# Three weight rings, alternating chunk products and earlier low-rank weights in an RWKV-7/Conformer block

## The chip, the cores and the metric

The kernel runs on one NeuronCore of a Trainium2 chip. The metric is the device time of one execution in microseconds (us). TensorE (PE) multiplies into PSUM, ScalarE (ACT) and VectorE (DVE) do the elementwise work, GpSimd (POOL) and SyncE (SP) issue transfers (DMA) between the chip's memory and SBUF.

## What is computed

One layer on x of 512 tokens by 1024 channels, in float32: a mixer of two branches, then a gated feed-forward network (FFN).

```
h = rms_norm(x); proj = h @ w_in                  # r, k, v, conv (2), z_rwkv, z_conv: 7 x 1024 columns
w = w0 + tanh(xw @ w1) @ w2;  a = sigmoid(a0 + (xa @ a1) @ a2);  g = sigmoid(xg @ g1) @ g2
...
S = S * w_t + (S @ a_t) b_t^T + v_t k_t^T;  y_t = S @ r_t          # wkv7: 16 heads of 64, over 512 steps
y_rwkv = (group_norm(y) + bonus) * g @ w_rwkv_out
y_conv = silu(layer_norm(depthwise_conv31(u * sigmoid(gate)))) @ w_conv_out
x = x + rms_norm((sigmoid(z_rwkv) * y_rwkv + sigmoid(z_conv) * y_conv) @ w_out)
h = rms_norm(x); f = (silu(h @ w_gate) * (h @ w_up)) @ w_down      # d_ff = 2816
x = x + rms_norm(f)
```

## The kernel before

**Products.** Channels lie on the partitions, the 512 tokens along the free axis. A float32 product is made of three products in the format fp32r: weights and data are each split into a high and a low part (`wh`, `wl`; `HH`, `HL`), and `acc3` adds `wh` by high, `wh` by low and `wl` by high. A product of 1024 inputs into 128 outputs ("a tile") thus takes 24 matmuls of 512 columns into one of two PSUM tiles `dn`; a tile of the down projection, with 2816 inputs, takes 66.

**Loads of weights.** A load is half a tile's weights: 128 by 512 numbers, 256 KB. `wload` (L436) knows two ways. By SP: a transfer into `wf`, ScalarE copies it into `wh`, VectorE subtracts and writes `wl` (`split`, L432). By POOL: a transfer into `wh`, ScalarE writes its negative into `wl`, and a second transfer adds the weights to `wl`. All of these tiles have the tag "w" in the pool `wp`, whose number of places is `WT` (12). `wres` (L1132) and `lastw` (L1342) take a `wf` of the same tag alone and split into tiles elsewhere that stay resident.

**The planned part.** Everything from the first keys to the last tile of `w_co` goes through the class `Sched`: it does not issue instructions at once, but collects them in streams, gives each a cost (`times`, L182), simulates the five engines and issues the instruction that can start first, by priority (a smaller number is more urgent). `order` then fixes this order for each engine. Products stand in `sc.items` as a tile with the events that it needs (`dense_tile`, L703); `feed` (L315) takes the first item in the list whose events are posted and keeps at most `WB` = 6 halves loaded ahead; all go through one stream "dense", in order. Loads go by SP until the event "open", then by POOL until the taps of the last convolution tile are planned, then by SP again.

For each pair of heads `ct` (0 to 7; two heads of 64 channels fill 128 partitions, `E` are the lower 64 rows, `O` the upper) there are `prep` (keys, decays, and `gps`: the products inside chunks of 64 tokens), `solve` (inverse of a triangular matrix, products on 16 and 32 rows such as `wqs`), `values`, `chain` (eight chunks, one after another) and `finish`. They call each other by events: `prep(ct)` posts ("keys", ct), ("tr", ct) and ("inner", ct), `values` posts ("val", ct). The tile of `v` for `ct` needs ("val", ct-1).

`gps` works in two halves `hc` of four chunks; in each it fills a PSUM tile for the head in `E` and then one for the head in `O` (both of the tag "sm", two places), four float32 products each of 64 rows, 128 outputs and 128 columns. Each PSUM tile is then read twice by ScalarE (into `Mt`) and twice by VectorE (into `AR`, `GR`).

`conv(ct)` makes two tiles (gate and value), `taps(ct)` the 31 taps of the depthwise convolution on VectorE. `norms` (L1086) writes the normalised input `HH`, `HL`, then splits the low-rank weights of g (`low_weights(1)`, into `wg`) and puts the item of `low_rank1` (48 matmuls `lora`) at the end of `sc.items`; when these are made, it posts "low1". The convolution tiles from `ct` = 1 on, and the taps, need "low1", because the tile "ca" first holds x, then `wg`, then the convolutions.

**The rest.** After `sc.run()` (L1234) the instructions are given in plain program order and the framework schedules them: five tiles of `w_o` (`dense`, L459), interleaved with `wres` for the first four gate/up tiles; three further tiles of `w_o` from resident weights; the residual and the first four gate/up tiles from resident weights (`psf`); 20 pairs of gate/up tiles (L1327); seven tiles of the down projection, with `lastw` for the eighth (L1355); the eighth tile in two halves of the tokens. For each pair of gate/up tiles VectorE does `sg` = gate * `bc`, ScalarE silu, VectorE `sg` * `bc` and `sg` * up, and ScalarE and VectorE split the result into `FH` (high and low). A down tile is evicted by ScalarE (`dn`, then its square).

The two ways of `wload` before the change:

```
if eng is G:
    wh, wl = (wp.tile([P, nk * P], F32R, tag="w", name=n_) for n_ in ("wh", "wl"))
...
    wf = wp.tile([P, nk * P], F32, tag="w", name="wf")
    wh, wl = (wp.tile([P, nk * P], F32R, tag="w", name=n_) for n_ in ("wh", "wl"))
```

Of the kernel before, what the change touches and what calls it, by code (L numbers as in the profile page):

```python
# [3 lines left out]

# [5 lines left out]
F32 = mybir.dt.float32  # L10
F32R = mybir.dt.float32r
# [6 lines left out]
P = 128  # L18
# [3 lines left out]
NT = D // P  # L22
# [7 lines left out]
KW = 31  # L30
WK = 4
WB = 6
WT = 12
LB = {"mu_r": 2, "mu_k": 2, "mu_v": 1}
NWO = 3
BUFS = (2, 2, 2, 2, 1, 1, 1)
# [45 lines left out]
def tile_hybrid_block(ctx, tc, xT, cst, prm, dwp, wl1, w2g, w_in, w_ro, w_co, w_o,  # L82
# [13 lines left out]
    class Sched:  # L96
# [85 lines left out]
        def times(self, eng, name, k, aps):  # L182

            out = aps[0]
            n = math.prod(out.shape[1:])
            if eng == "PE":
                lhsT, rhs = k["lhsT"], k["rhs"]
                n, m = math.prod(rhs.shape[1:]), math.prod(lhsT.shape[1:])
                if lhsT.dtype == F32R:
                    c = max(0.112, 0.452e-3 * n)  # L190
                elif name == "transpose":
                    c = 0.112
                elif m > 64:
                    c = 2 * max(0.112, 1.02e-3 * n)
                else:
                    c = 0.058 if m > 32 else 0.016
                return c, c + 0.17, 0.0
            if "dma" in name:
                size = P * n * 4 if out.shape[0] > 64 else 64 * n * 4
                land = 2.0 + size / 200e3  # L200
                if eng == "POOL":
                    return (0.91, 0.06, land + 0.7) if k.get("accum_op") else (0.65, 0.06, land + 0.3)
                return 0.06, 0.06, land
            psum = any(str(a.space) == "PSUM" for a in aps[1:])
            if eng == "ACT":
                t = 0.17 + 0.9e-3 * n - (0.03 if psum else 0)
                t += sum(0.08 for a in ("scale", "bias") if hasattr(k.get(a), "ap"))
                return t + 0.02, t, 0.0
            if eng == "POOL":
                return 0.2 + 1.2e-3 * n, 0.2 + 1.2e-3 * n, 0.0  # L210
            t = 0.16 + 1.035e-3 * n
            if name == "scalar_tensor_tensor":
                t += 0.05 if n > 64 else 0
            elif name == "transpose":
                t = 0.16 + 1.8e-3 * n
            elif name == "tensor_tensor_scan":
                t = 0.16 + 2.06e-3 * n
            elif name in ("tensor_scalar", "tensor_copy"):
                t = 0.15 + 0.75e-3 * n
            return t - 0.08, t, 0.0  # L220
# [139 lines left out]
    sc = Sched()  # L360
# [19 lines left out]
    PE, SY = Engine("PE", nc.tensor), Engine("SP", nc.sync)  # L380

    def pool(stack, name, bufs, **k):
        return Pool(stack.enter_context(tc.tile_pool(name=name, bufs=bufs, **k)), bufs)

    cp = pool(ctx, "cp", 1)
    wp = pool(ctx, "wp", WT)
    tp = pool(ctx, "tp", 1)
    sp = pool(ctx, "sp", 2)
    pd = pool(ctx, "pd", 2, space=PSUM)
    pm = pool(ctx, "pm", 2, space=PSUM)  # L390
# [38 lines left out]
    E, O = slice(0, 64), slice(64, 128)  # L429
# [5 lines left out]

    def wload(wap, nk, eng=None):  # L436
        if eng is G:
            wh, wl = (wp.tile([P, nk * P], F32R, tag="w", name=n_) for n_ in ("wh", "wl"))
            G.dma_start(out=wh, in_=wap)
            S.activation(out=wl, in_=f(wh), func=AF.Copy, scale=-1.0)  # L440
            with sc.stream("low"):
                G.dma_start(out=wl, in_=wap, accum_op=ALU.add)
        else:
            wf = wp.tile([P, nk * P], F32, tag="w", name="wf")
            wh, wl = (wp.tile([P, nk * P], F32R, tag="w", name=n_) for n_ in ("wh", "wl"))
            SY.dma_start(out=wf, in_=wap)
            split(wf, wh, wl)
        return wh, wl
# [200 lines left out]
    def low_rank1():  # L649
        t_ = low[1]  # L650
        d = {}

        def mm(k):
            if k == 0:
                d["ps"] = pd.tile([P, T], F32, tag="dn", name="lora")
            for q, rh, rl in ((0, hh, hl), (2, hhs, hls)):
                o = acc3(d["ps"], t_[:, q, k, :], t_[:, q + 1, k, :], [k], rh, rl,
                         k + q == 0, k == NT - 1 and q == 2)
            if k == NT - 1:
                lo_f = tmp("lo_f", "th")  # L660
                S.activation(out=lo_f, in_=d["ps"], func=AF.Tanh, scale=0.5)
                S.activation(out=lo_f, in_=lo_f, func=AF.Identity, scale=0.5, bias=0.5)
                split(lo_f, GH, GL)
                sc.post("low1")
            return o

        sc.items.append(((), lambda: [(lambda eng: None, [lambda k=k: mm(k) for k in range(NT)])]))

    def open_loop():
        nonlocal kp  # L670
# [75 lines left out]
    def prep(ct):  # L746
# [57 lines left out]
        AR = kp.tile([P, NCH, 3, L], F32, tag="AR", bufs=BUFS[0], name="AR")  # L804
        bk = kp.tile([P, NCH, 2 * L], F32, tag="bk", bufs=1, name="bk")
# [8 lines left out]
        for hc in range(2):  # L814
            ps = pm.tile([P, 4, P], F32, tag="sm", name="tps")
# [14 lines left out]
        GR = kp.tile([P, NCH, 2, L], F32, tag="GR", bufs=BUFS[1], name="GR")  # L830
        sm = lambda rows: m_str[rows].unsqueeze(1).to_broadcast([64, 4, L])
        for hc in range(2):
            for par in range(2):
                cc = slice(hc * 4, hc * 4 + 4)
                R, Q = ((E, O), (O, E))[par]
                ps = pm.tile([P, 4, P], F32, tag="sm", name="gps")
                for c in range(4):
                    PE.matmul(ps[:, c, :], lhsT=bk[R, hc * 4 + c, :],
                              rhs=AR[R, hc * 4 + c, par:3:2 - par, :], start=True, stop=True)
                r0 = R.start  # L840
                S.activation(out=Mt[r0:r0 + B32, cc, :], in_=ps[r0:r0 + B32, :, 0:L],
                             func=AF.Copy)
                S.activation(out=Mt[r0 + B32:r0 + L, cc, 0:B32],
                             in_=ps[r0 + B32:r0 + L, :, B32:L], func=AF.Copy)
                V.tensor_mul(AR[Q, cc, par, :], ps[Q, :, 0:L], sm(Q))
                V.tensor_mul(GR[:, cc, par, :], ps[:, :, L:2 * L],
                             m_inc.unsqueeze(1).to_broadcast([P, 4, L]))
# [183 lines left out]
    def conv(ct):  # L1031
        cv = {}

        def gate(ps):
            if ct == 0:
                ps = early(ps)
            cv["th"] = tmp("th")
            S.activation(out=cv["th"], in_=ps, func=AF.Tanh, scale=0.5)

        def value(ps):  # L1040
            if ct == 0:
                ps = early(ps)
            cb = conv_in[ct] = conv_place(ct) if ct else cpad0
            V.scalar_tensor_tensor(out=cb[:, KW - 1:], in0=cv["th"], scalar=1.0,
                                   in1=ps, op0=ALU.add, op1=ALU.mult)

        rh, rl = (hh, hl) if ct else ((lambda k: XH[:, k, :]), (lambda k: XL[:, k, :]))
        need = ("low1",) if ct else ()
        dense_tile(w_in[4 * NT + ct], gate, rh, rl, need)
        dense_tile(w_in[3 * NT + ct], value, rh, rl, need, ("cv", ct))  # L1050

# [34 lines left out]
    def norms():  # L1086
        normed()
        yield "rest"
        low_weights(1)
        low_rank1()  # L1090
# [15 lines left out]
    sc.fast = False  # L1106
    sc.spawn(once(first_keys), 2)
    sc.spawn(once(low_inputs), 1)
    sc.spawn(norms(), 3)
    conv(0)  # L1110
    for ct in range(1, NT):
        dense_tile(w_in[NT + ct], lerp_of("tk", D_OMK, "mu_k", ct), need=(("keys", ct - LB["mu_k"]),) if ct >= LB["mu_k"] else (),
# [2 lines left out]
                   need=(("val", ct - 2),) if ct > 1 else (), ev=("r", ct))  # L1115
# [16 lines left out]
    def wres(wap, hi, lo, j):  # L1132
        for k0 in range(0, NT, WK):
            c = slice(k0 * P, (k0 + WK) * P)
            o_ = slice(j * D + k0 * P, j * D + (k0 + WK) * P)
            wf = wp.tile([P, WK * P], F32, tag="w", name="wf")
            SY.dma_start(out=wf, in_=wap[:, c])
            split(wf, hi[:, o_], lo[:, o_])

# [81 lines left out]
    for m in range(NT):  # L1221
        dense_tile(w_in[6 * NT + m], lambda ps, m=m: gate_c(m, ps),
                   need=(("inner", NT - 1), ("val", NT - 1)))
# [25 lines left out]
    for m in range(NT - NWO):  # L1249
        ps = dense(w_o[m], mh, ml)  # L1250
# [91 lines left out]
    def lastw(i):  # L1342
        if i < 4:
            n = WK
            t_ = [kq.tile([P, WK * P], F32R, tag=QT[2 * i + h], bufs=QT.count(QT[2 * i + h]),
                          name="lw") for h in range(2)]
            wf = wp.tile([P, WK * P], F32, tag="w", name="wf")
            SY.dma_start(out=wf, in_=w_dn[NT - 1][:, i * WK * P:(i + 1) * WK * P])
            split(wf, *t_)
        else:  # L1350
            n = min(WK, NF - i * WK)
            t_ = wload(w_dn[NT - 1][:, i * WK * P:(i * WK + n) * P], n)
        last.append((n, *t_))

    for m in range(NT - 1):  # L1355
        ps = dense(w_dn[m], Fh, Fl)
# [7 lines left out]
    for h in range(2):  # L1364
        c = HALF[h]
        ps = pd.tile([P, TH], F32, tag="dn", name="dn")
# [82 lines left out]
```

## Time and profile before

| | |
|---|---|
| time, median of 3 runs | 1222.57 us (1222.13 to 1225.49) |
| profiled execution | 1221.62 us, its span 1219.6 us |
| busy share of the span | TensorE 91%, weight loads 72%, VectorE 61%, ScalarE 46%, GpSimd 8% |
| mean granted clock of TensorE | 0.958 of 2.4 GHz |
| transfers | 106.95 MB, mean 88 GB/s |

The span runs from the first to the last instruction of the profiled execution. Matmuls are pipelined and their ends are modelled, so that a busy TensorE is not one at its peak. The granted clock is a mean over a stretch; the clock itself has two levels, 1.2 and 2.4 GHz. Lines of the profile that end in brackets give the idle time of the engine just before the instruction and what ended it. In the planned part every instruction has the line L300, behind it L225, so that instructions are known by their tiles.

### The profile page before, as it was taken

The numbers are of one execution on the slowest core, as the hardware profiler recorded it, in microseconds if no ns is written. First come the engines' busy times: TensorE is split into PE (matmuls) and PEld (weight loads), VectorE is DVE, ScalarE is ACT, GpSimd is POOL, SyncE is SP. The second block draws the span as 40 slices with busy tenths as digits, with TensorE's granted clock in tenths as the row PEclk, the third lists the DMA queues.
The fourth block names the chain that finished last, engine by engine and source line by source line (L and its number), as shares of the span: only waits on it lengthen the run. The fifth ranks groups of instructions, "written<-read, shape, count | busy, mean of one in ns | idle before, by whom it ended". The sixth has DMA issues, their size and how long they took to land.

```text
span 1219.6 us, 18527 instructions
## 1 busy us (share of the span) xinstructions
PE 1115.1 (91%) x7066; PEld 883.2 (72%) x7066; DVE 741.5 (61%) x1507; ACT 562.7 (46%) x1199; POOL 100.3 (8%) x167
## 2 busy tenths in 40 slices
PE   6978999999999899899999998999988888888896
PEld 5756777777777677577788876988766666666676
DVE  6869888989899888867543553664443434412214
ACT  6456666667767665464742333542222222222211
POOL 0022222222122221000000000000000000000000
PEclk9888998989899998998999998999999999999998
DMA  6033544545354542222232243012222222322322
GB/s 236 22 74 72 118 81 93 113 92 111 71 111 81 125 88 55 67 84 87 83 99 95 95 144 98 18 44 92 91 69 86 69 87 70 92 79 81 91 72 69
DMA packets 68440, 106.95 MB, mean 88 GB/s; under 512 B 15104, under 2 KB 20608, under 8 KB 68352
## 3 DMA queue, kind: packets, MB, share of 16 engines
q1 hardware_dynamic: 49344, 71.16, 18.8%
q0 software_dynamic: 19008, 34.61, 14.1%
q8 instruction: 56, 0.92, 0.3%
q14 instruction: 32, 0.26, 0.1%
HBM read 101.55 MB, written 2.10 MB: 85 GB/s over the span
## 4 chain that ended last, share of the span: by engine, by line
PE 76%; DVE 13%; issue 5%; ACT 4%; DMA 2%; SPq 0%; POOL 0%; DVEq 0%; ACTq 0%; POOLq 0%
PE dn L225 31%; PE dn L300 26%; PE zt L300 5%; DVE cacc L300 3%; DVE wl L225 2%; PE psf L225 2%; PE lora L300 2%; PE gps L300 2%; PE wo L225 1%; DMA SV<-UV 1%; PE yp L300 1%; DVE AR L300 1%; ACT Mt L300 1%; DVE kkn L300 1%; DVE GR L300 1%
## 5 line engine op out<-in xcount | busy, mean ns | idle before, releaser
L300 PE MATMUL dn<-HH,wl 128*128 128x512 f32 x408 | 169.5, 415 | 4.1 <-DMA wl<-in_w_in_dram 4.1
L300 PE MATMUL dn<-HL,wh 128*128 128x512 f32 x408 | 172.6, 423 | 0.0
L300 PE MATMUL dn<-HH,wh 128*128 128x512 f32 x408 | 170.5, 418 | 0.0
L300 DVE SCALAR_TENSOR_TENSOR cacc<-ca,dw,cacc 128x512 f32<-128x512 f32 x203 | 151.7, 747 | 4.5
L225 PE MATMUL dn<-FHH,wl 128*128 128x512 f32 x320 | 129.2, 404 | 25.6 <-DVE wl L225 25.6
L225 PE MATMUL dn<-FHL,wh 128*128 128x512 f32 x320 | 127.0, 397 | 0.0
L225 PE MATMUL dn<-FHH,wh 128*128 128x512 f32 x320 | 126.2, 394 | 0.0
L225 DVE TENSOR_TENSOR wl<-wf,wh 128x512 fp32r<-128x512 f32 x140 | 91.5, 670 | 48.6 <-ACT wh L225 48.4
L225 PE MATMUL dn<-FH,wh 128*128 128x512 f32 (+1 forms) x332 | 105.3, 401 | 12.8 <-ACT wh L225 12.8
L225 ACT ACTIVATE wh<-wf 128x512 fp32r<-128x512 f32 x140 | 79.5, 609 | 39.6 <-PE dn L225 24.1
L225 PEld LDWEIGHTS dn<-FHH,wl 128*128 128x128 f32 x320 | 60.0, 188 | 50.8 <-DVE wl L225 37.8
L300 PEld LDWEIGHTS dn<-HH,wl 128*128 128x128 f32 x408 | 79.9, 196 | 18.8 <-DMA wl<-in_w_in_dram 4.2
L300 PEld LDWEIGHTS dn<-HH,wh 128*128 128x128 f32 x408 | 79.3, 194 | 14.7 <-issue 0.2
L300 PEld LDWEIGHTS dn<-HL,wh 128*128 128x128 f32 x408 | 79.8, 196 | 14.0 <-issue 1.0
L225 PEld LDWEIGHTS dn<-FH,wh 128*128 128x128 f32 x332 | 63.0, 195 | 28.7 <-ACT wh L225 15.4
L300 POOL DMA_DIRECT2D wl<-in_w_in_dram x66 | 58.0, 968 | 208.0 <-ACT wl L300 175.1
L300 DVE TENSOR_TENSOR wl<-wf,wh 128x512 fp32r<-128x512 f32 x72 | 49.5, 689 | 37.8 <-PE dn L300 20.9
L225 PEld LDWEIGHTS dn<-FHL,wh 128*128 128x128 f32 x320 | 60.1, 188 | 14.4
L225 PEld LDWEIGHTS dn<-FHH,wh 128*128 128x128 f32 x320 | 60.1, 188 | 13.7
L225 PE MATMUL dn<-FH,wl 128*128 128x512 f32 (+1 forms) x166 | 66.3, 399 | 1.6 <-DVE wl L225 1.6
L300 ACT ACTIVATE wh<-wf 128x512 fp32r<-128x512 f32 x72 | 44.5, 626 | 40.7 <-DVE wl L300 36.9
L225 DVE TENSOR_TENSOR sg<-sg,dn 128x512 f32<-128x512 f32 x20 | 13.7, 687 | 71.4 <-PE dn L225 71.3
(304 smaller groups left out, 2145.2 us busy)
## 6 DMA issues: line engine op xcount, KB each, us to landing
wh<-in_w_in_dram POOLq DMA_DIRECT2D x66, 256.0 KB, 4.1
wl<-in_w_in_dram POOLq DMA_DIRECT2D x66, 256.0 KB, 4.2
wf<-in_w_in_dram SPq DMA_DIRECT2D x46, 256.0 KB, 2.8
wf<-in_w_gt_dram SPq DMA_DIRECT2D x44, 256.0 KB, 2.7
wf<-in_w_up_dram SPq DMA_DIRECT2D x44, 256.0 KB, 2.7
wf<-in_w_dn_dram SPq DMA_DIRECT2D x40, 256.0 KB, 2.7
wf<-in_w_ro_dram SPq DMA_DIRECT2D x16, 256.0 KB, 2.6
wf<-in_w_co_dram SPq DMA_DIRECT2D x16, 256.0 KB, 2.6
```

Source lines behind the costliest of these rows:

```text
L225: return fn(*a, **k)
L300: i = fn(*a, **k)
```

## The change

Four things change. (1) The ring of twelve weight tiles becomes three rings of four (`WT` = 4 for each tag): loads by SP put `wf` into "w0", `wh` into "w1" and `wl` into "w2"; loads by POOL take the three rings in turn; a lone `wf` goes into "w0". (2) In `prep` both PSUM tiles of a half are taken first, and the products of the two heads alternate between the rows `E` and `O`; the reads follow, tile by tile. The planner's cost of a float32 product with more than 64 outputs changes: 0.224 us up to 128 columns, and 0.52 of the cost for products on 64 rows or fewer. (3) `norms` gets the priority 1 in place of 3, `low_rank1` puts its item at the front of the list and posts "lowq" at once. (4) The convolution tiles 1 to 4 need "lowq" in place of "low1", and the tiles 5 to 7 need ("inner", ct-1).

```diff
-WT = 12
+WT = 4
...
-                    c = 2 * max(0.112, 1.02e-3 * n)
+                    c = 2 * (0.112 if n <= P else 1.02e-3 * n) * (0.52 if lhsT.shape[0] <= 64 else 1)
...
+    turn = itertools.count()
...
         if eng is G:
-            wh, wl = (wp.tile([P, nk * P], F32R, tag="w", name=n_) for n_ in ("wh", "wl"))
+            wh, wl = (wp.tile([P, nk * P], F32R, tag=f"w{next(turn) % 3}", name=n_)
+                      for n_ in ("wh", "wl"))
...
         else:
-            wf = wp.tile([P, nk * P], F32, tag="w", name="wf")
-            wh, wl = (wp.tile([P, nk * P], F32R, tag="w", name=n_) for n_ in ("wh", "wl"))
+            wf = wp.tile([P, nk * P], F32, tag="w0", name="wf")
+            wh, wl = (wp.tile([P, nk * P], F32R, tag=f"w{i}", name=n_)
+                      for i, n_ in ((1, "wh"), (2, "wl")))
...
-        sc.items.append(((), lambda: [(lambda eng: None, [lambda k=k: mm(k) for k in range(NT)])]))
+        sc.items.insert(0, ((), lambda: [(lambda eng: None, [lambda k=k: mm(k) for k in range(NT)])]))
+        sc._post("lowq")
...
         for hc in range(2):
-            for par in range(2):
-                cc = slice(hc * 4, hc * 4 + 4)
+            cc = slice(hc * 4, hc * 4 + 4)
+            pss = [pm.tile([P, 4, P], F32, tag="sm", name="gps") for _ in range(2)]
+            for c in range(4):
+                for par, R in ((0, E), (1, O)):
+                    PE.matmul(pss[par][:, c, :], lhsT=bk[R, hc * 4 + c, :],
+                              rhs=AR[R, hc * 4 + c, par:3:2 - par, :], start=True, stop=True)
+            for par, ps in enumerate(pss):
                 R, Q = ((E, O), (O, E))[par]
-                ps = pm.tile([P, 4, P], F32, tag="sm", name="gps")
-                for c in range(4):
-                    PE.matmul(ps[:, c, :], lhsT=bk[R, hc * 4 + c, :],
-                              rhs=AR[R, hc * 4 + c, par:3:2 - par, :], start=True, stop=True)
...
-        need = ("low1",) if ct else ()
+        need = () if not ct else ("lowq",) if ct < 5 else (("inner", ct - 1),)
...
-    sc.spawn(norms(), 3)
+    sc.spawn(norms(), 1)
...
-            wf = wp.tile([P, WK * P], F32, tag="w", name="wf")
+            wf = wp.tile([P, WK * P], F32, tag="w0", name="wf")
```

The last pair of lines stands in both `wres` and `lastw`.

## Rows read from the trace of the kernel before

**Rows 1.** Busy time by stage: us, busy of each engine, PEclk (granted clock), DMA share, GB/s.

```profile
586.00:722.00 136.00, 135.93 (x584) 109.05 (x582) 66.14 (x101) 61.17 (x92) 0.00 (x0) 1.00 0.31 100
722.00:759.24 37.24, 30.13 (x115) 22.84 (x116) 11.16 (x18) 11.95 (x22) 0.00 (x0) 0.91 0.36 118
...
805.39:871.72 66.33, 66.33 (x285) 53.34 (x285) 31.63 (x50) 21.39 (x36) 0.00 (x0) 1.00 0.27 88
871.72:1062.94 191.22, 164.67 (x675) 123.99 (x673) 73.59 (x114) 47.48 (x86) 0.00 (x0) 1.00 0.25 77
1062.94:1175.68 112.74, 99.33 (x395) 76.52 (x395) 27.06 (x45) 27.93 (x54) 0.00 (x0) 0.95 0.31 87
```

**Rows 2.** Timeline of all engines, 862 to 902: start us, us, engine, line, operation.

```profile
861.69 0.39 PE L225 MATMUL dn<-FHH,wh 128*128 128x512 f32 x1
...
862.48 1.29 DVE L225 TENSOR_TENSOR wl<-wf,wh 128x512 fp32r<-128x512 f32 x2
...
866.09 0.69 DVE L225 TENSOR_TENSOR sg<-dn,bc 128x512 f32<-128x512 f32 x1 [2.32 <-PE dn L225]
...
871.69 0.69 DVE L225 TENSOR_TENSOR sg<-sg,dn 128x512 f32<-128x512 f32 x1 [2.92 <-PE dn L225]
871.72 0.40 PE L225 MATMUL dn<-FHL,wh 128*128 128x512 f32 x1
872.30 0.68 DVE L225 TENSOR_TENSOR wl<-wf,wh 128x512 fp32r<-128x512 f32 x1
...
873.01 1.72 SPq L225 DMA_DIRECT2D wf<-in_w_gt_dram  x2
...
873.03 0.50 PE L225 MATMUL dn<-FHH,wl 128*128 128x512 f32 x1 [0.91 <-DVE wl L225]
```

**Rows 3.** Waits of TensorE, 871 to 1062: us in total, times, longest.

```profile
PE dn L225 <- DVE wl L225: 25.6, 28, 0.9
```

**Rows 4.** Waits of TensorE, 1063 to 1200.

```profile
PE dn L225 <- ACT wh L225: 12.8, 6, 2.3
PE dn L225 <- DVE wl L225: 1.6, 5, 0.9
```

**Rows 5.** Waits of VectorE, 871 to 1062, the first line.

```profile
DVE sg L225 <- PE dn L225: 117.8, 29, 4.1
```

**Rows 6.** Timeline of ScalarE between two down tiles.

```profile
1078.15 0.69 ACT L225 ACTIVATE dn<-dn,pr 128x512 f32<-128x512 f32 x1 [9.61 <-PE dn L225]
...
1079.21 2.19 ACT L225 ACTIVATE wh<-wf 128x512 fp32r<-128x512 f32 x4
```

**Rows 7.** Timeline of all engines, 83 to 91: the first head pair.

```profile
83.33 1.71 PE L300 MATMUL gps<-AR,bk 64*128 64x128 f32 x16
84.53 0.37 ACT L300 ACTIVATE Mt<-gps 32x256 f32<-32x256 f32 x1 [1.78 <-PE gps L300]
...
86.15 1.16 PE L300 MATMUL gps<-AR,bk 64*128 64x128 f32 x8 [1.11 <-ACT Mt L300]
```

**Rows 8.** Tile `gps`: count, ns min/median/max, first and last start, forms.

```profile
L300 PE MATMUL gps<-AR,bk x256: 272/272/579, 83.3 to 470.7; 64*128 64x128 f32 x128
```

**Rows 9.** Timeline of TensorE, 104.5 to 110: the products on 16 rows.

```profile
105.39 0.75 PE L300 MATMUL wqs<-P32T,Mt 16*32 16x32 f32 x64
```

**Rows 10.** Busy time in three stretches of the planned part.

```profile
60.00:120.00 60.00, 45.87 (x385) 35.13 (x385) 46.51 (x110) 36.48 (x66) 14.12 (x24) 0.86 0.32 68
120.00:480.00 360.00, 347.12 (x3125) 274.35 (x3123) 319.20 (x740) 237.72 (x596) 85.47 (x135) 0.94 0.48 97
480.00:555.00 75.00, 65.91 (x587) 49.64 (x587) 59.48 (x114) 39.62 (x109) 0.00 (x0) 0.92 0.21 65
```

**Rows 11.** Timeline of TensorE, 55 to 120: its two longest waits.

```profile
79.61 0.80 PE L300 MATMUL lora<-HH,wg 128*128 128x512 f32 x1 [4.60 <-DVE wg L300]
...
115.47 0.79 PE L300 MATMUL dn<-HH,wl 128*128 128x512 f32 x1 [4.10 <-DMA wl<-in_w_in_dram]
```

**Rows 12.** Tile `cacc`: the last tap of convolutions 1 to 7.

```profile
L300 DVE SCALAR_TENSOR_TENSOR ca<-ca,dw,cacc x7: 711/752/755, 220.1 to 532.8; 128x512 f32<-128x512 f32 x7
```

More of the change, by code (lines that the diff above doesn't have):

```diff
@@ L1 @@
-import heapq
+import itertools
 import math
@@ L1346, in lastw @@
                           name="lw") for h in range(2)]
-            wf = wp.tile([P, WK * P], F32, tag="w", name="wf")
+            wf = wp.tile([P, WK * P], F32, tag="w0", name="wf")
             SY.dma_start(out=wf, in_=w_dn[NT - 1][:, i * WK * P:(i + 1) * WK * P])
```

## The prediction, made before the change was run

> **What bounds the kernel now.** I read the page first: TensorE is by far the busiest engine, so the end moves with the work taken off it and with the holes closed in it. Then the table by stage, to see where the holes are. The planned part (it ends near 722) closes with a stretch that has none, 135.93 us busy of 136.00. Behind it the first gate/up products have none either, 66.33 of 66.33; but w_o is busy 30.13 of 37.24, the other gate/up products 164.67 of 191.22 and the down tiles 99.33 of 112.74 [rows 1]. The same code runs without a hole for 12 gate/up products and then loses time on every one. What a product costs without a hole follows from two matmuls of the good stretch, at 861.69 and 871.72 [rows 2]: 43 steps in 10.03 us, 0.2333 us each, so 5.60 us for a product of 24 and 15.40 us for a down tile of 66.
>
> TensorE's waits name the holes: 28 for `wl`, 0.9 us each, in the gate/up stretch [rows 3]; in the down stretch 6 for `wh` of up to 2.3 us and 5 for `wl` [rows 4]. The queues tell why. VectorE idles 2.92 us until a product has ended, does `sg`, and only behind it the `wl` for which TensorE already stands, until 873.03; while there was no hole, the `wl` pair stood ahead of `sg` [rows 2]. It is not the load: VectorE's one wait worth listing there is for TensorE, 117.8 us [rows 5], and the `wf` transfers issued at 873.01, when that `wl` is done, are for later products [rows 2]. In the down stretch ScalarE idles 9.61 us until the tile has ended, evicts it, and only then makes four `wh` in one go [rows 6]. So the splits for the next product sit behind the eviction of this one: an order in a queue, not a lack of engine time (VectorE is busy 73.59 of 191.22 [rows 1]).
>
> Where that order comes from I read from the code, as the trace does not show it. In this part no order is written out, and the framework hands out the slots of one tag in program order. With one tag for `wf`, `wh` and `wl`, the `wf` of load n+1 comes after the `wl` of load n: in the framework's plan a load starts when the one before is split, the plan is load-bound, a product's end comes before the next splits, and the chip keeps that order though its transfers are early. The good stretch lives on the loads made while the resident products ran.
>
> **The change part by part.** My base is the profiled execution, 1221.62 us (its span of 1219.6 and 2.0 around it), 0.95 under the median of 1222.57.
>
> *Rings, gate/up.* Twelve places remain, four for each kind, but `wf` no longer queues behind `wl`: four transfers can run ahead, and `wh` and `wl` of load n+4 wait only for load n's last matmul, three loads (3 x 2.80 = 8.4 us) before their use. A split behind an eviction then costs nothing, being early. From 873.03 [rows 2] to the start of the down tiles at 1062.94 [rows 1], 28 products take 6.78 us each; at 5.60 that is 28 x 1.18 = 33 us less. Bounds: 0 if the order stays, and 35 if the first 12 are 5.53 as their stretch's 66.33 suggests.
>
> *Rings, down.* Six tiles take 112.74 us [rows 1], against 6 x 15.40 = 92.4: 20 us, of which 13.4 is idle and the rest matmuls after restarts (mean granted clock 0.95, so partly at 1.2 instead of 2.4 GHz). Bounds 0 and 20.
>
> *Rings, w_o.* Five products, 28.0 us, take the 37.24 of their stretch [rows 1]. The lone `wf` of `wres`, two per product, shifted the common ring; now they share `w0` with the loads, 4 transfers per product. I take the idle, 7 us; bounds 0 and 9.
>
> In the planned part the rings keep their depth (six pairs by POOL, four triples by SP), and its order is written out; I price them at nothing there, covered by loads that are six halves ahead.
>
> *Alternating products.* `gps` takes 32 matmul instructions per head pair. 16 in sequence need 1.71 us [rows 7], with the shortest single one at 0.27 [rows 8], so 96 ns each. Whether products on different rows run side by side, another group shows: 64 `wqs`, which go round four row quarters, take 0.75 us [rows 9], behind the same tail 8 ns each, where 32 columns at the rate of `gps` (128 columns) would be 24. At 96 ns the 256 of `gps` are 25 us of TensorE, and half of that is 12; at twice the price, where the clock is granted at its lower level, up to 18 in all. The lower bound is nothing: two PSUM tiles must now be evicted before the second half starts, and one eviction lasts from 84.53 to the next fill at 86.15, with TensorE waiting 1.11 us for it [rows 7]. I take 8, as dense products often lie ready to fill that wait. The Trainium skill (TensorEngine Tiling (Array Packing), PSUM Bottleneck) says that packing speeds TensorE but not the eviction, which may become the bound; by that this term is 0 and the time 1152. The 1.6 us of eviction per tile here against some 0.8 of halved products are on its side, unless other products fill in.
>
> *Low-rank weights.* From 60 to 120 TensorE idles 60 - 45.87 = 14.1 us, at a mean granted clock of 0.86 [rows 10]: it waits for `wg` and for a transfer [rows 11], while all conv products but the first are barred by "low1". Now those 48 products (11.2 us) stand in front, `normed` and the `wg` splits go ahead of `prep` on ScalarE and VectorE, and eight conv tiles may fill the hole. The 11.2 us only move. I take 10 of the 14. Against it: `prep(0)` is put behind those splits, and the `v` tile of head pair 1 may find six loaded halves ahead of it in the dense queue, 6 x 2.80 = 17 us. Bounds: 17 lost, 14 gained. The taps may start earlier; they are VectorE work, busy 319.20 of 360 from 120 to 480 [rows 10], and no shorter.
>
> *Held conv products* (5 to 7). They can fill holes later: from 480 to 555 TensorE idles 9.1 us [rows 10]. But the last tap starts at 532.8 [rows 12], and a product held too long makes taps later. I take 0; bounds 5 lost, 9 gained. The planner's new costs change only its order, within these bounds.
>
> Sum: 33 + 20 + 7 + 8 + 10 + 0 = 78; 1221.62 - 78 = 1143.6, and 0.95 more for the median: 1144. In the 136 us before 722 and in the tail behind 1176 nothing changes.
>
> **The rivals.**
> *The planned part gives nothing.* The loop over head pairs may be held by its chain of small products and evictions and by VectorE, with `v` late by up to 17. For it: from 120 to 480 TensorE's holes are 12.9 us of 360 and VectorE has 41 left at all [rows 10]. Time: 1222 - 60 = 1162, with the 17 lost 1179.
> *All of it.* 18 + 14 + 9 and 9 in w_o: 1222 - 33 - 20 - 9 - 41 = 1119.
> *The order stays.* If the splits stand behind the evictions for another cause, the rings gain nothing: 1222 - 18 = 1204. The Trainium skill (Perfetto Trace Analysis, Optimization Strategy) puts a gap that repeats down to too little memory for the next tile, buffer count or tile size; twelve places stay twelve, and by that rule the holes stay too, which is this rival's time. The good stretch speaks against the count and for the order: with the same twelve places it has no hole [rows 2].
> *Slower: splits too far ahead.* If the freed order puts a `wl` that needs a matmul of the next product in front of `sg`, the eviction comes a load (2.8 us) late. With two PSUM tiles that is free up to one product (5.6 us); beyond it TensorE stands for a load in each of 40 products: 40 x 8.4 = 336 us against 12 x 5.6 + 28 x 6.78 = 257, so 79 more. With 20, 7 and 18 gained elsewhere: 1256. Against it: the `sg` of an earlier product is earlier in the program when both are ready.
>
> **How the numbers follow.** My forecast 0.54 (1130 to 1161); the planned part gives nothing 0.22; all of it 0.10; the order stays 0.10, a fifth of that within 0.3%, should the planned part lose 17; slower 0.04. About 0.3% (3.7 us) is what a measurement of this kernel tells from no change. So faster 0.94, same 0.02, slower 0.04. The first three hold 0.86: the range goes from 1115 (all, with the 35) to 1182 (nothing, with the delay).
>
> **What would show it.** Right: TensorE's waits for `wl` and `wh` behind 805 nearly gone, 40 products at 5.6 us and down tiles at 15.4, each `wl` a product ahead of its use; 16 `gps` in about 1 us; TensorE idle under 5 us from 60 to 120, with conv products there. Wrong: `wl` still starts behind `sg` with TensorE idle; `gps` of the eight head pairs spread over more than the 83.3 to 470.7 of now [rows 8]; taps that start after 533 and hold up the normalisation.

## The result, and the profile after

The changed kernel takes 1136.62 us (median of four runs, 1133.89 to 1138.75), the kernel before 1223.80 beside it: a ratio of 0.9286, 95% interval 0.9256 to 0.9316. Forecast were 1144, with a range of 1115 to 1182. The profiled execution spans 1132.9 us, 86.7 less than before's 1219.6, and its mean granted clock is 0.974 instead of 0.958.

First the windows of the changed kernel, cut at the first matmuls of its stages (us, busy time and instructions of PE, PEld, DVE, ACT and POOL, granted clock, DMA share, GB/s): the planned part from 30 us on, the stretch from 60 to 120, the end of the planned part, w_o with five loaded and then three resident products, the resident gate/up products, the 40 loaded ones, and the down tiles in two pieces.

```profile
30.00:697.51 667.51, 635.04 (x4905) 496.26 (x4905) 532.84 (x1127) 405.23 (x911) 105.36 (x167) 0.96 0.40 94
60.00:120.00 60.00, 59.20 (x285) 46.76 (x285) 48.91 (x115) 36.23 (x64) 17.81 (x29) 1.00 0.48 103
552.10:697.51 145.41, 144.48 (x633) 116.46 (x632) 75.54 (x119) 69.18 (x106) 0.00 (x0) 1.00 0.31 99
697.51:725.50 27.99, 27.99 (x121) 22.56 (x120) 17.07 (x26) 16.48 (x30) 0.00 (x0) 1.00 0.63 198
725.50:746.90 21.40, 21.34 (x175) 20.58 (x174) 7.81 (x22) 9.13 (x20) 0.00 (x0) 1.00 0.07 22
746.90:771.60 24.70, 24.69 (x208) 24.48 (x206) 16.56 (x42) 10.52 (x22) 0.00 (x0) 1.00 0.00 1
771.60:996.30 224.70, 224.70 (x966) 180.65 (x966) 110.24 (x168) 78.71 (x125) 0.00 (x0) 1.00 0.28 92
996.30:1103.90 107.60, 107.60 (x463) 86.73 (x462) 33.44 (x52) 33.32 (x58) 0.00 (x0) 1.00 0.33 94
1103.90:1124.00 20.10, 18.50 (x153) 17.94 (x152) 7.16 (x24) 4.37 (x9) 0.00 (x0) 1.00 0.16 53
```

Read the span beside the busy time of PE: from 697.51 to 1103.90 they are the same, and the clock is 1.00. The 28 waits for `wl` of [rows 3] and the 11 of [rows 4] are gone; these are all of TensorE's waits behind 697:

```profile
PE bc L225 <- DVE rs L225: 1.0, 1, 1.0
PE psn L225 <- ACT sqf L225: 0.5, 1, 0.5
```

The queue shows how. In VectorE's timeline of the changed kernel (start, us, engine, line, operation, idle time before it and its releaser) `wl` still stands right behind `sg`, as in [rows 2], and is still made after it:

```profile
843.01 0.69 DVE L225 TENSOR_TENSOR wl<-wf,wh 128x512 fp32r<-128x512 f32 x1 [1.20 <-ACT wh L225]
845.33 0.69 DVE L225 TENSOR_TENSOR sg<-dn,bc 128x512 f32<-128x512 f32 x1 [1.63 <-PE dn L225]
845.94 0.68 DVE L225 TENSOR_TENSOR wl<-wf,wh 128x512 fp32r<-128x512 f32 x1
...
848.61 0.69 DVE L225 TENSOR_TENSOR wl<-wf,wh 128x512 fp32r<-128x512 f32 x1 [1.19 <-ACT wh L225]
```

What differs is whose weights they are: here a later load's, so that nobody waits for the pair behind `sg`. Counted through the trace, load by load, a `wl` is done 7.5 us before the first matmul that reads it; in the kernel before, that matmul (873.03 in [rows 2]) started as soon as it was.

Where the 86.7 us came from, by spans between the same instructions of the two profiled executions:

| stretch | before | after | less by | forecast |
|---|---|---|---|---|
| start to the first matmul of w_o | 718.36 | 697.51 | 20.9 | 18 (8 + 10 + 0) |
| w_o, five loaded and three resident products | 60.7 | 49.4 | 11.3 | 7 |
| resident gate/up | 24.5 | 24.7 | -0.2 | 0 |
| 40 gate/up products | 257.8 | 224.7 | 33.1 | 33 |
| down, to TensorE's last matmul | 149.7 | 127.7 | 22.0 | 20 |
| behind it | 8.5 | 8.9 | -0.4 | 0 |

### The profile page after: what moved, and what is told of

Read it like the earlier page. It is cut to its first block, busy times and chain, and to the rows that moved or that the text cites. A ratio compares the mean times of both kernels' runs of the same rounds, so it can differ in the third digit from the quotient of the medians.

```text
span 1132.9 us, 18576 instructions
## 1 busy us (share of the span) xinstructions
PE 1080.3 (95%) x7066; PEld 865.5 (76%) x7066; DVE 745.1 (66%) x1503; ACT 573.8 (51%) x1199; POOL 106.0 (9%) x175
## 4 chain that ended last, share of the span: by engine, by line
PE 84%; issue 7%; DVE 4%; ACT 2%; DMA 1%; POOL 1%; SPq 0%; DVEq 0%; POOLq 0%; ACTq 0%
PE dn L225 35%; PE dn L300 29%; PE zt L300 5%; PE lora L300 2%; PE psf L225 2%; PE gps L300 2%; PE wo L225 2%; PE yp L300 1%; PE vps L300 1%; PE psn L225 1%; PE tps L300 1%; POOL wl L300 1%; ACT Mt L300 1%; PE ssy L300 1%; POOL wh L300 0%
## 5 line engine op out<-in xcount | busy, mean ns | idle before, releaser
L225 ACT ACTIVATE wh<-wf 128x512 fp32r<-128x512 f32 x140 | 86.7, 619 | 217.8 <-PE dn L225 207.3
L300 PE MATMUL dn<-HL,wh 128*128 128x512 f32 x408 | 168.4, 413 | 0.0
L300 PE MATMUL dn<-HH,wh 128*128 128x512 f32 x408 | 167.7, 411 | 0.0
L225 PE MATMUL dn<-FHH,wl 128*128 128x512 f32 x320 | 127.7, 399 | 0.0
L225 PE MATMUL dn<-FH,wh 128*128 128x512 f32 (+1 forms) x332 | 101.3, 388 | 0.0
L300 POOL DMA_DIRECT2D wl<-in_w_in_dram x70 | 61.8, 931 | 262.9 <-ACT wl L300 188.4
L300 ACT ACTIVATE wh<-wf 128x512 fp32r<-128x512 f32 x68 | 42.3, 628 | 74.0 <-PE dn L300 69.4
L225 PE MATMUL dn<-FH,wl 128*128 128x512 f32 (+1 forms) x166 | 64.0, 385 | 0.0
L300 POOL DMA_DIRECT2D wh<-in_w_in_dram x70 | 45.6, 718 | 36.9 <-PE dn L300 36.1
```

Source lines behind the costliest of these rows:

```text
L225: return fn(*a, **k)
L300: i = fn(*a, **k)
```

## The experiments

Times are medians; "before" was run beside each set and took 1224.01, 1223.20 and 1222.90 us. Two kinds of question stood open: whether the rings close the holes by the order they allow or by something else, and what each edit of the planned part gives.

**The rings alone** (`rings_only`): the kernel before with

```
-WT = 12
+WT = 4
...
-            wh, wl = (wp.tile([P, nk * P], F32R, tag="w", name=n_) for n_ in ("wh", "wl"))
+            wh, wl = (wp.tile([P, nk * P], F32R, tag=f"w{i}", name=n_)
+                      for i, n_ in ((1, "wh"), (2, "wl")))
```

and the other ring lines of the change.

> The kernel before with the three rings and nothing else of the change. Theory (the order of the splits in the queues): the gate/up products from the thirteenth on take 5.60 us instead of 6.78, the down tiles 15.4 instead of 18.8, w_o about 30 us instead of 38, TensorE's waits for wl and wh in these stretches are gone, and the planned part still ends near 721: 1222 - 60 = 1162 us. If the rings give part of the planned part's gain too, below 1155. Rival (the order stays, and the gain after the planned part came from another edit): 1222 us, with the 28 waits for wl.

Measured: 1160.68 us, ratio 0.9483 (0.9454 to 0.9512), 63 us less. The windows of w_o, gate/up and down:

```profile
721.60:749.60 28.00, 28.00 (x121) 22.57 (x120) 16.88 (x26) 16.34 (x29) 0.00 (x0) 1.00 0.62 198
749.60:771.00 21.40, 21.34 (x176) 20.59 (x175) 7.83 (x22) 9.10 (x20) 0.00 (x0) 1.00 0.07 23
...
795.70:1020.40 224.70, 224.70 (x966) 180.68 (x966) 110.24 (x168) 78.62 (x125) 0.00 (x0) 1.00 0.28 91
1020.40:1148.10 127.70, 126.08 (x615) 104.71 (x613) 40.61 (x76) 37.66 (x67) 0.00 (x0) 1.00 0.30 88
```

These are the changed kernel's numbers to a tenth. Everything won behind the planned part is the rings'; the planned part ends 3.2 us later than before (721.60).

**Everything but the rings** (`all_but_rings`): the changed kernel with one ring of twelve, those lines turned back.

> The changed kernel with one ring of twelve places instead of three of four. Theory: the planned part keeps its gain and ends near 698, and what follows takes the 498.4 us that it took before (721.2 to 1219.6), with the waits for wl and wh back: 698 + 498 + 2 = 1198 us. If the planned part's gain needs the rings, its end is near 721 and the time near 1220. Rival (the rings do nothing): 1137.

Measured: 1198.05 us, ratio 0.9791 (0.9759 to 0.9824). All holes are back, the same ones:

```profile
779.70:1037.50 257.80, 232.18 (x967) 178.48 (x967) 104.45 (x164) 68.43 (x121) 0.00 (x0) 1.00 0.25 80
1037.50:1187.00 149.50, 133.67 (x615) 107.16 (x613) 40.07 (x78) 36.29 (x69) 0.00 (x0) 0.97 0.27 78
```

The planned part ended at 692.59 here, earlier than with the rings.

**One ring, but transfers written ahead** (`one_ring_ahead`): the slots stay twelve in one ring; only the text of the gate/up products takes `wf` of later loads before the `wh` and `wl` of this one.

```
+            wf = got.pop(0) if got else fetch(wap)
+            while ahead and len(got) < 2:
+                got.append(fetch(ahead.pop(0)))
             wh, wl = (wp.tile([P, nk * P], F32R, tag="w", name=n_) for n_ in ("wh", "wl"))
-            SY.dma_start(out=wf, in_=wap)
             split(wf, wh, wl)
```

`fetch` takes the place and starts the transfer; `ahead` lists the gate/up loads.

> The kernel before, one ring of twelve; only in the gate/up products the program text takes the place of a load's wf, and starts its transfer, two loads before the split that uses it, so that wf of load n+2 stands ahead of wh and wl of load n. Slots, their count and their sizes stay. Theory (places of one tag are handed out in program order, and this order is the whole cause): the gate/up holes close as with the rings, 28 x 1.18 = 33 us, while the down tiles stay at 18.8: 1222 - 33 = 1189 us. Rival (one common tag of twelve places is too little memory, whatever the text's order): 1222 us with the 28 waits.

Measured: 1182.33 us, ratio 0.9669 (0.9628 to 0.9710). Gate/up, then down:

```profile
804.70:1029.30 224.60, 224.60 (x965) 180.54 (x966) 110.95 (x169) 77.55 (x125) 0.00 (x0) 1.00 0.28 92
1029.30:1171.00 141.70, 131.00 (x615) 106.44 (x614) 37.92 (x74) 35.22 (x66) 0.00 (x0) 0.98 0.27 80
```

Without a ring more, the gate/up holes close as with three. The gain is 41.7 instead of 33 us, because the lead built up lasts into the down tiles: 8.0 us less there, until it is used up and 8.7 us of waits for `wh` return. So it is the order in which places are handed out, and not the number of rings. (In this edit a transfer's start moves ahead together with its place; in the rings the text's order stays and only the places differ.)

**Nine places** (`rings_of_three`): `rings_only` with `WT = 3`.

> As rings_only, but three places in each ring, nine in all. Theory (order): gate/up products still at 5.60 us without waits for wl, down tiles 15.4 to 16; w_o, with four transfers per product through three places, and the planned part, which loads six halves ahead, may lose up to 30 us: 1162 to 1192 us. Rival (the count of places makes the holes): products slower than the 6.78 us of twelve places in one ring, over 1222 us.

Measured: 1156.11 us in its one run. W_o's two pieces, gate/up and down:

```profile
716.77:746.20 29.43, 29.43 (x120) 23.68 (x121) 15.99 (x24) 16.23 (x28) 0.00 (x0) 0.95 0.53 172
746.20:767.60 21.40, 21.34 (x175) 20.54 (x175) 8.38 (x23) 9.66 (x21) 0.00 (x0) 1.00 0.15 48
792.40:1017.10 224.70, 224.70 (x967) 180.67 (x967) 110.17 (x168) 78.67 (x126) 0.00 (x0) 1.00 0.28 92
1017.10:1145.00 127.90, 126.04 (x615) 104.68 (x613) 41.91 (x77) 38.74 (x68) 0.00 (x0) 1.00 0.31 90
```

Three quarters of the memory, and no hole in gate/up or down: the rival of buffer count has fallen. The lead is shorter: a `wl` is done 4.6 us before its first matmul, where four places gave 7.5. W_o's loaded products take 29.43 instead of 28.00 us in this one execution, at a mean clock of 0.95.

**The alternating products, with the planner's new costs and with the old ones** (`alternating_only`, `alternating_old_cost`): the kernel before with the new `gps` loop, and, in the first only,

```
-                    c = 2 * max(0.112, 1.02e-3 * n)
+                    c = 2 * (0.112 if n <= P else 1.02e-3 * n) * (0.52 if lhsT.shape[0] <= 64 else 1)
```

> The kernel before with the alternating gps products (both PSUM tiles taken ahead) and the planner's cost for matmuls on 64 rows, and nothing else. Theory (two row halves overlap): 16 gps take 1.16 us, as in the profile of the changed kernel, instead of 1.71; 16 such runs are 8.8 us less of TensorE, the planned part ends some 9 us earlier and the time is 1213 us. Rival (the evictions and VectorE's chain bound the loop over head pairs): the 16 gps are shorter, but the planned part ends within 2 us of where it did, 1222 us.

> The kernel before with the alternating gps products and the planner's old cost for them. alternating_only took 1206.0 us, 17 less than before: 11.8 of it is busy time of gps (36.85 to 25.02). Theory (the rows' overlap is the gain, and the planner's cost only orders): 1206 to 1211 us. Rival (the order that the new cost gives brings the rest): at least 1211, up to before's 1223.

Measured: 1205.98 us with the new costs (ratio 0.9861, 0.9844 to 0.9877) and 1226.88 with the old ones (1.0037, 1.0018 to 1.0057): 17 faster and 4 slower, with the same products. The planned part from 30 us to the first matmul of w_o, with the new costs:

```profile
30.00:700.97 670.97, 631.70 (x4905) 495.86 (x4905) 527.32 (x1119) 401.94 (x906) 108.42 (x171) 0.96 0.40 93
```

and with the old ones:

```profile
30.00:723.91 693.91, 646.64 (x4904) 503.25 (x4905) 532.52 (x1125) 401.89 (x908) 99.86 (x159) 0.94 0.37 88
```

From 120 to 360 us, new costs first, then old:

```profile
120.00:360.00 240.00, 238.03 (x2191) 187.07 (x2190) 219.17 (x495) 165.98 (x414) 68.83 (x106) 1.00 0.58 116
120.00:360.00 240.00, 227.89 (x2130) 176.55 (x2131) 211.63 (x480) 156.94 (x391) 60.09 (x93) 0.95 0.50 100
```

Three of TensorE's waits in the loop with the old costs (us, times, longest):

```profile
PE zt L300 <- ACT zs L300: 8.7, 9, 1.9
...
PE gps L300 <- ACT Mt L300: 4.5, 5, 2.1
PE wqs L300 <- DVE P32T L300: 4.1, 2, 4.0
```

The busy time of `gps` fell in both, from 36.85 before to 25.02 (new) and 28.59 us (old). With the old costs TensorE idles 693.91 - 646.64 = 47.3 us of the planned part, 8.8 more than before (688.36 - 649.89 = 38.5), and the eighth head pair's last `gps` starts at 486.8 instead of 470.7 [rows 8]; with the new costs at 453.5. Of the 8.3 us that `gps` saves there, only 3.3 are left in the busy time of the whole planned part (646.64 against 649.89). With the new costs the idle time is as before, 39.3 us, and the busy time is 18.2 shorter: 11.8 of `gps`, the rest at a mean clock of 0.96 instead of 0.94. Between the two costs lie 8.0 us of idle time and 14.9 of busy time, for the same products.

**The low-rank weights early, alone** (`lowrank_only`): the kernel before with

```
-    sc.spawn(norms(), 3)
+    sc.spawn(norms(), 1)
...
-        need = ("low1",) if ct else ()
+        need = ("lowq",) if ct else ()
```

and the `insert(0, ...)` and `_post("lowq")` of the change.

> The kernel before with the second low-rank weights urgent (priority 1, their products in front, the convolutions from 1 to 7 waiting for the queueing of these products alone, none held). Theory: TensorE's idle time between 60 and 120 falls from 14.1 to some 4 us and the planned part ends 10 us earlier, 1212 us. Rival (the v product of head pair 1 comes late, up to 17 us): the gps of the second head pair start after 143.6 and the time is up to 1239 us. Rival (VectorE's taps set the end, earlier work only waits longer): 1222 us.

Measured: 1204.21 us, ratio 0.9846 (0.9817 to 0.9875), 19 less. The hole from 60 to 120, and the whole planned part:

```profile
60.00:120.00 60.00, 58.38 (x457) 46.75 (x456) 49.13 (x117) 35.39 (x65) 18.46 (x30) 0.97 0.47 101
...
30.00:696.67 666.67, 641.79 (x4904) 508.42 (x4905) 532.45 (x1128) 402.67 (x908) 97.76 (x155) 0.96 0.39 91
```

The 14.1 us idle of [rows 10] are 1.6 here.

**Both of them, one ring, no hold** (`both_one_ring`): the two edits above together, with the new costs.

> The kernel before with the alternating products, their cost, and the urgent low-rank weights, without rings and without the hold. Alone the two were worth 17 and 19 us. If they add: 1223 - 36 = 1187 us. If they fill the same holes (the changed kernel's planned part ends only 21 to 26 earlier than before's): 1197 us.

Measured: 1191.00 us, ratio 0.9759 (0.9708 to 0.9809), 32 less of the 36 that would be the sum. They nearly add.

**The changed kernel without the hold** (`all_but_hold`):

```
-        need = () if not ct else ("lowq",) if ct < 5 else (("inner", ct - 1),)
+        need = ("lowq",) if ct else ()
```

> The changed kernel with convolutions 5 to 7 free as soon as those from 1 to 4 are. Theory of the prediction: holding them is worth nothing, 1137 us, and the taps end where they did (549.8) or earlier. If the hold makes the taps late: the last tap starts near 533 again and the time is 1132 us or less. If the hold fills holes late in the planned part: TensorE idles more from 480 to 555 and the time is up to 1146 us.

Measured: 1128.86 us, ratio 0.9227 (0.9210 to 0.9245): 7.8 us faster than the changed kernel, the fastest of all. Two windows without the hold:

```profile
240.00:360.00 120.00, 115.98 (x1090) 91.84 (x1090) 106.24 (x246) 82.71 (x209) 33.13 (x52) 0.99 0.54 109
360.00:480.00 120.00, 107.18 (x1238) 83.59 (x1236) 103.08 (x260) 82.18 (x222) 14.88 (x28) 0.91 0.28 61
```

and the same two in the changed kernel:

```profile
240.00:360.00 120.00, 109.61 (x1021) 83.81 (x1022) 107.29 (x253) 84.10 (x208) 26.24 (x41) 0.96 0.44 90
360.00:480.00 120.00, 114.93 (x1278) 89.04 (x1277) 103.26 (x250) 80.97 (x220) 25.14 (x43) 0.96 0.44 92
```

The hold moves a hole: TensorE idles 10.4 us from 240 to 360 with it (35 weight transfers issued by POOL, at 90 GB/s) against 4.0 without (45, at 109 GB/s), and 5.1 against 12.8 in the next window. Over the whole planned part the idle times are nearly equal, 32.5 us with the hold and 31.8 without. What differs is TensorE's busy time for the same 4905 recorded matmuls, 635.0 against 630.3, at a mean clock of 0.96 against 0.97. The normalisation's sums start at 552.1 instead of 548.8, behind a last tap at 550.5 instead of 547.1. Which of the two costs the time is not shown.

**The changed kernel without the alternation and its costs** (`all_but_alternating`).

> The changed kernel with the gps products one half after the other, and the planner's old cost, as before. Theory: 16 runs of 16 cost 0.55 us more each, 8.8 us in all, and lie on TensorE's path: 1146 us. Rival (the loop is bound by evictions and VectorE): 1137 us.

Measured: 1150.06 us, ratio 0.9401 (0.9384 to 0.9417), 13.4 more than the changed kernel, where 8.8 were expected from the runs of 16 alone.

**Without the hold, with the old costs** (`no_hold_old_cost`): the alternating products stay.

> The changed kernel without the hold (1128.9 us) and with the planner's old cost for matmuls on 64 rows. If the cost only orders: 1127 to 1131 us. If the new cost brings part of the gain: 1132 us or more.

Measured: 1138.49 us, ratio 0.9317 (0.9268 to 0.9366), 9.6 more than with the new costs.

**Without the hold, three places in each ring** (`no_hold_three`).

> The changed kernel without the hold (1128.9 us) and with three places in each ring. Three places had no hole in gate/up and down, and the planned part ended 4.8 us earlier than with four: 1124 to 1130 us. Rival (with the planned part shorter, nine places are too few for loads six halves ahead): 1135 us or more.

Measured: 1148.27 us, ratio 0.9396 (0.9360 to 0.9431), 19 more: a miss. W_o starts at 710.72 instead of 692.02 here, though with the old order of the planned part it ended 4.8 us earlier with three places (716.77) than with four (721.60), in one execution each. Of the 18.7 us in the planned part 7.9 are idle time (39.7 against 31.8) and 10.8 busy time of the same 4905 recorded matmuls, at a mean clock of 0.94 instead of 0.97. So the time is the rival's: nine places lose time in the planned part of this kernel, where the old order showed no such loss. Which load it is was not traced.

## Why the prediction was right, and where it was off

*The order of the splits* (33, 20 and 7 of 78) holds. The cause that could only be read from the code, places of one tag handed out in program order, was tested by writing the order by hand in one ring: 224.6 us for the 40 products, as with three rings (224.7), against 257.8. The Trainium skill (Perfetto Trace Analysis, Optimization Strategy) says that a gap that repeats can mean too little memory for the next tile; it does not say that it must, as the prediction has it. Here it did not: nine places in order have no holes, twelve out of order have them all. Gate/up came to 33.1 and down to 22.0; the bound of 20 was worked out for six down tiles, and the stretch measured holds all eight. "The order stays" and "slower: splits too far ahead" are out.

*W_o* was mis-sized: 7 forecast with an upper bound of 9, 11.3 measured. I took the idle time for the term. Before, the 60.74 us from w_o's first matmul to its last hold 53.55 us of busy time, so 7.2 idle; after, the same products are busy 27.99 + 21.34 = 49.33. The other 4.2 are matmuls that no longer run at the lower granted clock (0.91 in the stretch of [rows 1], 1.00 now). In the down term I had counted both, here only the one. The upper bound of 9 was short for a second reason: it is 37.24 less 28.0, and that stretch begins at 722, while w_o's first matmul is at 718.36.

*Rings in the planned part, nothing.* Nearly: a few us lost. Its end, in one execution each, is 3.2 later alone, in the changed kernel 697.51 against 692.59 with one ring, without the hold 692.02 against 693.63; but that last 693.63 (`both_one_ring`) is from an execution of 1199.73 us, 8.7 above its kernel's median. The medians of whole times have one sign: the rings are worth 63.3, 61.4 and 62.1 us in these three pairs, where the stretches behind the planned part give 66, so some 3 to 5 are lost in it.

*Alternating products, 8, with the planner's costs at nothing.* Here the step failed in its cause, though 17 alone and 13 taken out of the changed kernel lie inside the bound of 18. TensorE's share came out, 11.8 us less busy `gps` where half of 25 had been worked out, but by luck: `gps` was busy 36.85 us before, not 25. The 96 ns each were read off 16 products that already overlap in part; eight on one half alone take 1.16 us [rows 7], and 16 alternating take the same 1.16 (last section). And "the planner's new costs change only its order, within these bounds" (5 lost, 9 gained) is wrong: they were put at nothing and decide the sign. With the old costs the alternation is worth 4 us less than nothing; with the new ones beside the alternation it is 21 us faster in the kernel before, and 9.6 in the kernel without the hold. The reading of the Trainium skill (TensorEngine Tiling (Array Packing), PSUM Bottleneck) by which the eviction becomes the bound (the section says that it may, after a fourfold speed-up of TensorE) made the term 0, and with the old costs that comes nearest. Yet TensorE's waits before `gps`, which [rows 7] has waiting for its own eviction, did not grow (10.4 us before, 7.2 with the old costs, 5.0 with the new); those that grew stand before the later products `zt`, and by as much with either cost (5.3 us before, 15.4 and 15.1), so PSUM is not shown to be the place, and these waits do not tell the costs apart. A possible reading, from the code alone: a run of 16 matmul instructions is 8 products in the plan, and the old cost lets them take 8 x 0.261 = 2.1 us, where the chip takes 1.16 (the new cost: 0.93), so that the work behind them is ordered for a time that never comes. But the edit also lowers the price of every float32 product of 128 rows and 128 columns, `zt` among them, from 0.261 to 0.224. Which of the two prices makes the better order, and whether the new costs would gain as much with the halves one after the other, was not run and stays open.

*Low-rank weights, 10, at most 14.* Mis-sized: 19 alone. The bound of 14.1 was TensorE's idle time, and its busy time fell too: in the planned part idle by 13.6 us and busy by 8.1 (from 649.89 to 641.79), for as many recorded matmuls (4905 and 4904). The likely reason is the clock, 0.96 in the mean where it was 0.94. I had the row for it, the clock of 0.86 in the stretch [rows 10], and counted only the hole, as in w_o. The 17 us for a late `v` did not come: the second head pair's `gps` start at 142.3, before they were at 143.6.

*The hold, 0, bounds 5 lost and 9 gained.* It lost 7.8, just beyond; the argument that held products fill holes from 480 to 555 failed: TensorE idles 7.4 us there with the hold and 5.7 without. They fill one from 360 to 480 and leave one from 240 to 360 that is nearly as long. The mark that I named for being wrong, taps that start after 533, was met: the last starts at 550.5 and the sums stand behind it. It is mostly not the hold's doing (547.1 without it; 521.2 in `lowrank_only`, 546.6 in `alternating_only`).

Put together, the planned part gave 20.9 where 18 was forecast: the two edits together 31.9 (17 and 19 alone), less 7.8 for the hold and some 4 for the rings. That the total was near is partly luck of these signs. The ends of the range, added up again from the terms, are 1117 and 1179 instead of 1115 and 1182; the result lies inside either.

The planned part as a whole, from 30 us to the first matmul of w_o, in one profiled execution each (whole times of one kernel here lie up to 11 us apart, so a few us between two rows say nothing; the execution of `both_one_ring` was 8.7 us slower than its median):

| kernel | us | TensorE busy | idle | mean clock |
|---|---|---|---|---|
| before | 688.4 | 649.9 | 38.5 | 0.94 |
| `alternating_old_cost` | 693.9 | 646.6 | 47.3 | 0.94 |
| `alternating_only` | 671.0 | 631.7 | 39.3 | 0.96 |
| `lowrank_only` | 666.7 | 641.8 | 24.9 | 0.96 |
| `both_one_ring` | 663.6 | 632.9 | 30.7 | 0.96 |
| after | 667.5 | 635.0 | 32.5 | 0.96 |
| `all_but_hold` | 662.0 | 630.3 | 31.8 | 0.97 |

Each row is 4904 or 4905 recorded matmuls. The busy time holds the clock as well as the products: `lowrank_only` shortens no product and has 8.1 us less of it. A shorter product lowers it; whether that reaches the first column is for the order to decide.

## What to carry to other kernels

Where an engine waits for an operand whose input has long arrived, look at what stands ahead of it in the producer's queue, and at the order in which its buffers are handed out, before adding buffers: separate tags for the stages of one pipeline, or the next transfer written ahead in the text, do it with the same memory or less. When a scheduler's cost table is corrected together with an operation, price the table as an edit of its own and measure them apart. And hold work back only if the place where it was running doesn't become the new hole: compare the two windows, not the one that is to be filled.

## What the runs showed of the hardware

Filling a hole in TensorE's work paid more than the hole. From 60 to 120 before's granted clock was 0.86, a mean over its two levels of 1.2 and 2.4 GHz, with 14.1 us idle; in `lowrank_only`, with 1.6 us idle, it was 0.97, in the changed kernel, with 0.8 us idle, 1.00, and `lowrank_only` was 19 us faster. W_o shows the same: 7.2 us of holes closed, 11.3 gained.

Products on different row halves overlap fully when they alternate. Eight `gps` on one half alone take 1.16 us, and 16 with one half after the other take 1.71 and not twice 1.16, as the second half starts before the first has ended [rows 7]; 16 alternating, in the timeline of the changed kernel:

```profile
237.07 1.16 PE L300 MATMUL gps<-AR,bk 64*128 64x128 f32 x16
```

That is the time of the eight: in the records of this run the two matmuls of a pair start 7 ns apart, and the pairs follow each other at 0.11 us, as single ones on one half do.
